# New DMA and port estimates in the planner that orders a two-layer hybrid backbone on one core

## The chip, the cores and the metric

The kernel runs on one core of a Trainium2 chip. A core has a matrix engine (TensorE, PE in the profile, with its weight loads as PEld), a vector engine (VectorE, DVE), an activation engine (ScalarE, ACT), GpSimd (POOL) and a queue processor (SyncE, SP) that issues DMA transfers here. Each takes its instructions in program order and waits on semaphores for the others. The metric is the device time of one execution in microseconds, as the median of several runs; lower is better.

## The reference, cut to what matters

Two layers work on 2048 latent tokens and 256 context tokens of width 1024. Each layer normalises its input, projects it, runs two groups of heads on the same projection (windowed softmax attention with eight heads, and a two-way mLSTM with four heads), gates both, and multiplies the joined result with one output matrix.

```python
def hybrid_layer(x, ctx, mod_x, mod_c, tables, norm_g, w_in, ..., last):
    xn = rmsnorm(x, norm_g) * (1 + scale_x) + shift_x
    cn = rmsnorm(ctx, norm_g) * (1 + scale_c) + shift_c
    aq, ak, av, az, mq, mk, mv, mo, mz, mi, mf = project(xn, w_in)
    ...
    att_x = window_ctx_attention(q, k, v, kc, vc, sink) * jax.nn.silu(az)
    cq, ck = mlstm_qk(cmq, cmk, conv_w, conv_b)
    xq, xk = mlstm_qk(mq, mk, conv_w, conv_b)
    h_ctx, ctx_state = mlstm_bidir(cq, ck, cmv, cmi + b_i, cmf + b_f, mlstm_init_state(B))
    h_lat, _ = mlstm_bidir(xq, xk, mv, mi + b_i, mf + b_f, ctx_state)
    m_x = mlstm_post(h_lat, mo, mz, head_g)
    out_x = jnp.concatenate([att_x, m_x], axis=-1) @ w_out
    x = x + gate_x * out_x
    if not last:
        ...
    return x, ctx

def reference(x, c, ctx, c_ctx, w_ada, b_ada, norm_g, w_in, ...):
    ...
    for l in range(DEPTH):
        ...
        x, ctx = hybrid_layer(...)
    return rmsnorm(x, final_g)
```

## The kernel before

Tokens are cut into 18 blocks of 128: two of context, sixteen latent. Every large product is done in three fp16 passes over high and low parts of the operands (`mm3`, line 350: 24 matmuls for one result), and the activations of a layer lie in SBUF as such pairs, transposed, in five group buffers `xt0` to `xt4`.

**The planner.** Nothing in the code is in the order in which it is issued. The class `Plan` (line 87) runs while the program is built. The work is written as generators. A *stream* yields pieces of TensorE work; a *task* carries the evacuation and the elementwise work that follow a piece. Each engine has a clock, E, V, S, G and Q for TensorE, VectorE, ScalarE, GpSimd and SP's DMA issues. `op` (line 147) estimates when an instruction starts and ends (`cost`, line 116), moves the engine's clock, notes from when on its result can be read and its buffer can be written, and then emits the real instruction (line 179; every instruction carries this line in the profile, so that one reads it by tiles). The planner's present is the clock of TensorE.

`till` (line 233) holds a stream or a task back until the estimate says that its operand is ready within 0.2 us. `get` (line 190) holds it back until the buffer it asks for is estimated free within 0.5 us, 0.2 us in PSUM. `put` (line 222) gives a buffer back with the latest time noted for it; for a buffer that a DMA reads this is the DMA's estimated landing. When all streams are held back, the clock of TensorE jumps to the earliest time that one waits for. So an estimate changes no instruction; it changes in which order the instructions of an engine come, and the engines then run in that order with real semaphores.

`run_until` (line 253) takes tasks first and then one piece of the first stream that is not held back: weight loads (priority -1), then keys and values, gates and out-projection (1), then alpha, beta and adaLN (2). Streams of one priority are sorted by the TensorE time they have used over their weight: alpha has `W_ALPHA` = 308, beta 560.

**Alpha** (line 1203) is the attention, four units of two heads in each layer. For each block of 128 queries it emits two *scores* (line 1064, one for each head), the gate projection `zproj` and, one block later, `pv` (line 1120), the product with the values; every second block also `qproj`. A score's task (line 1087) takes the row maximum on VectorE in a PSUM buffer `d` (two of them), the exponential on ScalarE, writes the high part of the probabilities to `ph` on ScalarE and the low part on VectorE, gives `d` back, and has SP transpose `ph` into `pp` by DMA. There is one buffer `ph`, for up to 1280 columns (twice five blocks of 128), and three `pp`. `ph` is free again when the transpose has landed.

**Beta** (line 1614) is the mLSTM, four heads in each layer: `mproj` (line 1210: projections, a five-tap convolution on GpSimd and VectorE, forward states) and `mmix` (line 1385: outputs in the order of the backward scan). `mmix` reads queries, gate rows and states from DRAM scratch by DMA (`p<-qD`, `mb<-mD`, `s<-cfD`).

**Joining.** The out-projection (`outproj`, line 1648) of a block needs that block's output of all heads, which goes through DRAM (`mixD`). Its weights are loaded by the stream `wo` (line 1896). It starts when beta's last `mproj` is done, when the weights of beta's last `mmix` are loaded, and when alpha's last unit has set the flag "wa soon" (line 1194), eight blocks, that is sixteen scores, before its end; it also needs the group buffers `xt4` and `xt3`, which alpha's and beta's last unit free (`clear`, line 1624). Alpha's last unit and `outproj` take the latent blocks in the same falling order. Layer 1 starts from what `outproj` of layer 0 puts into its group buffers, with DMA transposes of 2048 columns (`norm_dma`, line 675, and `prep`, line 1729).

**Lanes.** The program's DMAs take eight semaphores in turn; a DMA is issued when the one eight before it has landed.

The lines that the change touches: `__init__` (line 91), the branches of `cost` for "Q" and for VectorE (lines 124 to 145), and `op` from line 162 to line 171.

Of the kernel before, what the change touches and what calls it, by code (L numbers as in the profile page):

```python
# [7 lines left out]
F16 = mybir.dt.float16  # L8
# [5 lines left out]
P = 128  # L14
D = 1024
# [38 lines left out]
def _isap(v):  # L54
    return hasattr(v, "ap") and hasattr(v, "offset")
# [9 lines left out]
def _span(v):  # L65
    """Name and range of the bytes of one partition (or of DRAM) that v covers."""
    dims = list(v.ap)
    size = 2 if v.dtype == F16 else 4
    off = v.offset
    if v.space != bass.MemoryType.DRAM:  # L70
        step = dims[0][0]
        off = off % step if step else off
        dims = dims[1:]
    lo = hi = off
    for st, n in dims:
        if st < 0:
            lo += st * (n - 1)
        else:
            hi += st * (n - 1)
    return v.name, lo * size, (hi + 1) * size  # L80


W_ALPHA = 308.0
LAT, WAR = 0.12, 0.12


class Plan:
    """The order of emission.  Streams and tasks are generators: they yield True after a piece of work,
    a time to wait for, or None while a flag or a buffer is missing.  The engines' times are estimated."""

    def __init__(self):
        self.clk = dict(E=0.0, V=0.0, S=0.0, G=0.0, Q=0.0)
        self.dma = 0.0
        self.wr, self.rd, self.bank_of = {}, {}, {}
        self.done, self.tasks, self.streams = set(), [], []
        self.spec, self.cnt, self.rel, self.tag_of = {}, {}, {}, {}
# [4 lines left out]

# [1 line left out]
    def _times(self, table, v):  # L103
# [12 lines left out]
    def cost(self, e, name, a, kw):  # L116
# [7 lines left out]
        if e == "Q":  # L124
            b = n * a[0].shape[0] * (2 if a[0].dtype == F16 else 4)
            if name == "dma_start_transpose":
                return 0.8, 2.2 + b / 300e3
            return 0.46, 2.0 + b / 300e3
        if name == "tensor_reduce":
# [11 lines left out]
        if name == "reciprocal":  # L141
            n *= 8
        if name == "tensor_copy" and a[0].dtype == F16:
            n /= 2
        return 0.065 * (1 + min(cols, 2)) + n / 960.0, LAT

    def op(self, e, name, fn, a, kw):
# [13 lines left out]
        for v in ins + outs:  # L161
            for f, x in self.bank_of.get(v.name, {}).items():
                if f != e:
                    t = max(t, x)
        end = t + cost
        self.clk[e] = end
        see = end + lat
        if e == "Q":
            b = (lat - 2.0)
            self.dma = max(self.dma, end) + b  # L170
            see = self.dma + 2.0
        for v in outs:
# [7 lines left out]

# [1 line left out]
    def buffers(self, tag, pool, shape, dtype, bufs, psum=False):  # L182
# [17 lines left out]
    def take(self, tag, n, shape=None, dtype=None):  # L200
        """n buffers at once."""
        while True:
            if self.cnt[tag] + n > self.spec[tag][3]:
                yield None
            elif sorted(self.rel[tag])[n - 1] > self.now + 0.5:
                yield sorted(self.rel[tag])[n - 1]
            else:
                return [self.new(tag, shape, dtype) for _ in range(n)]
# [22 lines left out]

# [1 line left out]
    def till(self, *aps, slack=0.2):  # L233
# [74 lines left out]
class Kern(Plan):  # L308
# [33 lines left out]

# [1 line left out]
    def mm(self, out, lhsT, rhs, start=True, stop=True):  # L344
# [5 lines left out]
    def mm3(self, out, lh, rh, step=6):  # L350
        """Three passes over pairs: lh, rh give the operand of (hi or lo, k)."""
        c = 0
        yield from self.till(lh(0, 0), lh(1, KT - 1), rh(0, 0), rh(1, KT - 1))
        for k in range(KT):
            for a, b in ((0, 0), (0, 1), (1, 0)):
                self.mm(out, lh(a, k), rh(b, k), start=(k == 0 and a + b == 0), stop=(k == KT - 1 and a == 1))
                c += 1
                if c % step == 0 and c < 3 * KT:
                    yield True

# [1 line left out]
    def open(self, es):  # L362
# [44 lines left out]

# [1 line left out]
    def consts(self):  # L409
# [29 lines left out]

# [1 line left out]
    def scale_of(self, src, n=1, s=None, inv=None):  # L441
        """s = 2^14 / 2^floor(log2 src) and 1 / s, per partition."""
        V = self.V
# [9 lines left out]
    def pmax(self, am, out):  # L453
        """out = maximum over partitions of am [P, 1], on every partition."""
        yield from self.till(am)
# [5 lines left out]

# [1 line left out]
    def load_w(self, key, pieces, tag, scale=None, gate=(), gram=False, early=False, fast=False, space=None, into=None):  # L463
        """pieces: dram aps [D, n <= 128].  u: the product's unit.  With gram: the power of two that
        brings products of the first 128 columns under 2^15 (Cauchy-Schwarz), and u over it."""
        V, S, G, Q = self.V, self.S, self.G, self.Q
# [80 lines left out]

# [1 line left out]
    def ada(self, l, parts, width, tags):  # L549
        """Rows (g (1 + scale), shift, gate) of both streams to modD; the scale of xn."""  # L550
        A, Q, V = self.A, self.Q, self.V
# [73 lines left out]

# [1 line left out]
    def rstd(self, ss, scale, eps, n=1, out=None):  # L627
        """(ss * scale + eps) ^ -1/2 with one Newton step."""
        V, G = self.V, self.G
# [13 lines left out]
    def norm_pe(self, l, b, xr, free=None):  # L643
        """xr [P, D] of block b, normed and modulated, to the pairs XT of layer l."""
        S, V = self.S, self.V
# [29 lines left out]
    def norm_dma(self, l, b, xr, grab):  # L675
        """norm_pe with the turn done by DMA."""
        g, o = self.grp(b)
# [15 lines left out]
    def split(self, pair, x, s):  # L693
        """x times the column s as the pair of fp16 parts."""
        yield from self.till(x, s)
# [93 lines left out]

# [1 line left out]
    def rope(self, u, n, tok):  # L791
        """u [P, n] of latent tokens tok .. tok + n, turned in place."""
        V, G = self.V, self.G
# [12 lines left out]

# [1 line left out]
    def kphase(self, l):  # L808
# [67 lines left out]

# [1 line left out]
    def rphase(self, l):  # L878
# [106 lines left out]

# [1 line left out]
    def attention(self, l, j):  # L987
# [220 lines left out]

# [1 line left out]
    def mproj(self, l, h):  # L1210
# [172 lines left out]

# [1 line left out]
    def mmix(self, l, h):  # L1385
# [245 lines left out]
    def move_wo(self, l):  # L1631
        """The weights of the out-projection, from the room of the next layer's XT to their own."""
        yield from self.need(("alpha", l), ("mmix", l, MH - 1), ("wo", l, 3))
# [12 lines left out]

# [1 line left out]
    def outproj(self, l):  # L1648
# [59 lines left out]
        def scaled(gt, s):  # L1708
            """The gate with the units of the weights in it."""
            for n in range(4):  # L1710
# [34 lines left out]
        def grab(i):  # L1745
            """A buffer for a pair, and what gives it back: in the room of an XT, or a slot."""
            while True:
# [110 lines left out]

# [1 line left out]
    def loaders(self):  # L1860
# [49 lines left out]

# [1 line left out]
    def run(self):  # L1912
# [73 lines left out]
```

## Time and profile before

| what | us |
|---|---|
| median of 3 runs | 2785.13 |
| fastest and slowest run | 2782.59, 2791.67 |
| span of the profiled execution, first to last instruction | 2804.1 |

The profiled execution is one more execution of the same program, with the profiler on; its span is the only time that the profile gives for it. From first to last instruction it is 19.0 us (0.7%) longer than the median run. TensorE was granted 0.966 of its full clock on average over the span.

The page gives busy time by engine, the chain of work that ended last, and groups of instructions; a group is named by the tile that is written, "<-", and the tiles that are read. Other views show the instructions in order of time, the waits by who waited for whom, and the busy time in chosen stretches. A row of waits gives the total, how often, and the longest one. In the timeline, "[0.95 <-DMA pp<-ph]" says that the engine stood idle for 0.95 us and that the landing of the DMA from `ph` to `pp` ended it.

### The profile page before, as it was taken

What the parts mean: (1) busy time and instruction counts of PE and PEld (TensorE: products, weight loads), DVE (VectorE), ACT (ScalarE), POOL (GpSimd) and SP (SyncE); (2) the same over time, 40 slices, a digit from 0 to 9 for tenths busy, and PEclk for the clock granted to TensorE, in tenths of its full rate; (3) what the DMA queues carried; (4) which work ended last, traced back from release to release, by engine and by line L of the source; (5) the groups of instructions that cost most, each with busy time, mean ns of one, the idle gap of its engine ahead of it and who ended that gap; (6) DMA issues with size and microseconds to landing.
All of it is one profiled execution on the core that took longest, in us unless ns stands there. A gap on an engine that the chain in (4) does not pass through costs nothing. (4 is left out here: it accounts for less than half of the span.)

```text
span 2804.1 us, 64646 instructions
## 1 busy us (share of the span) xinstructions
PE 2470.3 (88%) x23650; PEld 1890.5 (67%) x23650; DVE 1850.9 (66%) x4817; ACT 1488.1 (53%) x3788; POOL 1515.6 (54%) x2832
## 2 busy tenths in 40 slices
PE   6789899988999899888799888998898899988898
PEld 2766786678668776775355558867785787677443
DVE  4878566756575656567677676657666665757775
ACT  1546565556566655565222356655674566556421
POOL 1846476637654765275322563775577367637321
PEclk8899999999999999999899999999999999999999
DMA  8344663577446634578888636633663675267775
GB/s 265 116 130 107 139 137 84 102 147 142 111 93 146 134 58 120 116 140 198 220 209 199 153 79 123 134 84 88 144 114 96 110 137 102 62 123 164 186 190 163
DMA packets 822448, 376.16 MB, mean 134 GB/s; under 512 B 492537, under 2 KB 800241, under 8 KB 821105
## 3 DMA queue, kind: packets, MB, share of 16 engines
q1 hardware_dynamic: 822128, 372.02, 59.2%
q8 instruction: 186, 3.05, 0.5%
q14 instruction: 134, 1.09, 0.1%
HBM read 198.99 MB, written 57.56 MB: 91 GB/s over the span
## 5 line engine op out<-in xcount | busy, mean ns | idle before, releaser
L179 PEld LDWEIGHTS <-xt 128*128 128x128 f16 x12048 | 901.8, 99 | 246.2 <-issue 51.0
L179 PE MATMUL b<-woz,xt 128*128 128x256 f16 (+2 forms) x3840 | 490.8, 277 | 24.8 <-DVE p L179 13.4
L179 PE MATMUL b<-xt,wqk 128*128 128x512 f16 (+1 forms) x1824 | 390.8, 367 | 1.4 <-DVE held L179 1.4
L179 DVE SCALAR_TENSOR_TENSOR ph<-d,ph 128x640 f16<-128x640 f32 (+2 forms) x272 | 212.3, 781 | 133.3 <-ACT ph L179 131.8
L179 ACT ACTIVATE d<-d,smx,un 128x640 f32<-128x640 f32 (+2 forms) x272 | 223.4, 821 | 126.4 <-DVE smx L179 113.4
L179 PEld LDWEIGHTS <-wqk 128*128 128x128 f16 x1824 | 176.9, 99 | 167.0 <-issue 11.2
L179 PE MATMUL d<-ks,toz 128*128 128x256 f16 (+1 forms) x1568 | 190.8, 258 | 92.8 <-DVE ph L179 62.8
L179 POOL TENSOR_TENSOR p<-p 128x128 f32<-128x128 f32 x272 | 128.6, 475 | 254.2 <-ACT p L179 240.5
L179 PE MATMUL b<-wa,xt 128*128 128x128 f16 (+1 forms) x3336 | 250.1, 226 | 4.0 <-ACT toz L179 3.1
L179 POOL TENSOR_TENSOR held<-held,mhalf 128x1 f32<-128x1 f32 x200 | 115.9, 580 | 240.5 <-DVE held L179 234.7
L179 PEld LDWEIGHTS <-toz 128*128 128x128 f16 x1568 | 148.1, 100 | 139.8 <-issue 54.8
L179 PE MATMUL b<-wv,xt 128*128 128x128 f16 x3456 | 228.9, 220 | 11.3 <-DVE p L179 5.3
L179 ACT ACTIVATE ph<-d 128x640 f16<-128x640 f32 (+2 forms) x272 | 182.0, 669 | 93.3 <-DMA pp<-ph 91.7
L179 DVE CUSTOM_DVE_ANT_0 d<-d,mask 128x640 f32<-128x640 f32 (+1 forms) x240 | 196.0, 817 | 36.4 <-PE d L179 35.8
L179 POOL TENSOR_TENSOR g<-g,mb 128x512 f32<-128x512 f32 (+1 forms) x152 | 189.0, 1243 | 39.4 <-ACT g L179 28.0
L179 PE MATMUL b<-xt,wa 128*128 128x256 f16 x1632 | 198.2, 275 | 4.1 <-DVE toz L179 1.9
L179 POOL TENSOR_TENSOR mb<-mb,mask 128x256 f32<-128x256 f32 x136 | 100.9, 742 | 177.0 <-DMA mb<-mD 143.5
L179 POOL TENSOR_TENSOR toz<-toz,cs 128x256 f32<-128x256 f32 x160 | 125.3, 803 | 105.3 <-DMA cs<-in_rope 83.1
L179 PEld LDWEIGHTS <-wa 128*128 128x128 f16 x1696 | 163.7, 99 | 27.2 <-issue 5.5
L179 DVE TENSOR_REDUCE held<-g 128x1 f32<-128x1024 f32 x110 | 133.1, 1212 | 62.8 <-DMA g<-mixD 34.4
L179 PE MATMUL b<-xt,xt 128*128 128x512 f16 x768 | 169.9, 382 | 5.3 <-DMA xt<-xt 3.2
L179 DVE SCALAR_TENSOR_TENSOR g<-g,cw 128x512 f32<-128x512 f32 (+1 forms) x152 | 152.4, 1002 | 31.4 <-POOL g L179 28.5
(243 smaller groups left out, 5200.1 us busy)
## 6 DMA issues: line engine op xcount, KB each, us to landing
mb<-mD SPq DMA_DIRECT2D x136, 256.0 KB
g<-in_w_in SPq DMA_DIRECT2D x60, 512.0 KB
cs<-in_rope SPq DMA_DIRECT2D x80, 256.0 KB
mixD<-p SPq DMA_DIRECT2D x272, 64.0 KB
g<-mixD SPq DMA_DIRECT2D x34, 512.0 KB
g<-in_w_ada SPq DMA_DIRECT2D x32, 512.0 KB
g<-in_x SPq DMA_DIRECT2D x24, 512.0 KB
cfD<-s SPq DMA_DIRECT2D x136, 64.5 KB
```

The source lines that it names most:

```text
L179: fn(*a, **kw)
```

## The change

It replaces estimates. No instruction, buffer, weight or priority is edited; docstrings and comments go, too.

- A plain DMA was estimated at 0.46 us of SP's time, and at 2.0 us plus its bytes over 300 GB/s from the end of the issue to the landing, transfers one behind another. It becomes 0.49 us of SP's time; the transfer may begin 0.3 us after the start of the issue and takes a time by the number and size of its contiguous runs; then 1.5 us pass to the landing where it writes DRAM, 1.9 us where it reads a kernel input, 3.6 us where it reads DRAM scratch or SBUF into SBUF.
- A DMA transpose was 0.8 us of SP's time, then 0.2 us and its bytes over 300 GB/s as a transfer, then 2.0 us. It becomes 1.2 us and 0.45 ns for each column over 512 as SP's time, a transfer of 25 ns for each column over sixteen engines, begun at the end of the issue, and 1.9 us.
- Eight DMAs are under way at most: a DMA starts no earlier than the landing of the one eight before it.
- A VectorE instruction with two operands of more than one column in SBUF, and every GpSimd instruction, exclude each other in time: the planner remembers the last six such stretches of each, and moves the start behind them.
- `tensor_tensor_reduce` (the row maximum in a score) costs 0.25 us plus a column per 960 MHz cycle, where it had 0.065 us for itself and for each column operand.

```diff
+def _run(v):
+
+    size = 2 if v.dtype == F16 else 4
+    r = size
+    for st, n in reversed(list(v.ap)):
+        if n == 1:
+            continue
+        if st * size != r:
+            break
+        r *= n
+    return r
+
+
+def _move(out, in_):
+
+    b = 2 if out.dtype == F16 else 4
+    for d in out.shape:
+        b *= d
+    r = max(min(_run(out), _run(in_), 4096), 4)
+    return b / r * (10 + 0.0447 * r) / 16e3
+
+
+def _base(out, in_):
+
+    if out.space == bass.MemoryType.DRAM:
+        return 1.5
+    return 1.9 if in_.name.startswith("in_") else 3.6
+
+
+def _two(a, kw):
+
+    n = 0
+    for v in list(a[1:]) + [v for k, v in kw.items() if k != "accum_out"]:
+        n += _isap(v) and _free(v) > 1 and v.space != bass.MemoryType.PSUM
+    return n > 1
...
         self.dma = 0.0
+        self.lanes, self.port = [0.0] * 8, dict(V=[], G=[])
...
         if e == "Q":
-            b = n * a[0].shape[0] * (2 if a[0].dtype == F16 else 4)
             if name == "dma_start_transpose":
-                return 0.8, 2.2 + b / 300e3
-            return 0.46, 2.0 + b / 300e3
+                return 1.2 + max(n - 512, 0) * 0.00045, 1.9 + n / 128 * 128 * 25e-3 / 16
+            return 0.49, _base(a[0], a[1]) + _move(a[0], a[1])
...
+        if name == "tensor_tensor_reduce":
+            return 0.25 + n / 960.0, LAT
...
+        if e == "Q":
+            t = max(t, self.lanes.pop(0))
+        elif e == "G" or (e == "V" and _two(a, kw)):
+            other = self.port["V" if e == "G" else "G"]
+            for p, q in other:
+                if p <= t < q:
+                    t = q
+            self.port[e] = self.port[e][-5:] + [(t, t + cost)]
         end = t + cost
         self.clk[e] = end
         see = end + lat
         if e == "Q":
-            b = (lat - 2.0)
-            self.dma = max(self.dma, end) + b
-            see = self.dma + 2.0
+            turn = name == "dma_start_transpose"
+            base = 1.9 if turn else _base(a[0], a[1])
+            self.dma = max(self.dma, end if turn else t + 0.3) + lat - base
+            see = max(self.dma + base, end)
+            self.lanes.append(see)
```

## The prediction, made before the changed kernel was timed

> **What bounds the kernel now.** I read the page first (span, engines, chain), then TensorE's waits, then the time of one score in the timeline, then what the last out-projection starts on.
>
> ```profile
> span 2804.1 us, 64646 instructions
> PE 2470.3 (88%) x23650; PEld 1890.5 (67%) x23650; DVE 1850.9 (66%) x4817; ACT 1488.1 (53%) x3788; POOL 1515.6 (54%) x2832
> PE b L179 6%; DMA pp<-ph 3%; DMA mb<-mD 2%; DMA g<-mixD 2%; DVE g L179 1%; DVE held L179 1%; POOL mb L179 1%; DMA g<-in_w_in 1%; PE d L179 1%; SPq L179 1%; POOL g L179 1%; DVE ph L179 1%; DVE xt L179 1%; POOL p L179 1%; ACT d L179 1%
> ```
>
> TensorE is the busiest engine, and 2804 - 2470 = 334 us of its span are idle. No estimate can save more than these. Of all transfers the attention's transpose (`pp<-ph`) has the largest part of the chain. The waits of TensorE say what the idle time is:
>
> ```profile
> PE d L179 <- DVE ph L179: 62.8, 67, 4.5
> PE b L179 <- DMA pp<-ph: 29.5, 28, 2.3
> PE d L179 <- DVE toz L179: 26.9, 12, 4.5
> PE b L179 <- DMA p<-qD: 19.0, 8, 4.7
> ```
>
> The planner holds a piece back until it believes the operand ready, so each such wait is an estimate that was too early. The first two, 62.8 + 29.5 = 92 us, belong to a score's tail: a buffer `d` is given back by the instruction that writes the low half of `ph`, and `pv` needs `pp`. Behind both stands the single buffer `ph`:
>
> ```profile
> ACT ph L179 <- DMA pp<-ph: 91.7, 83, 3.3
> ```
>
> ```profile
> L179 SPq DMA_TRANSPOSE pp<-ph x272: 1189/1342/6842, 205.0 to 2737.4; - x136
> ```
>
> In 83 of 272 scores ScalarE came to write `ph` before the transpose of the score before had landed. The timeline shows one such cycle:
>
> ```profile
> 1963.23 0.70 ACT L179 ACTIVATE ph<-d 128x640 f16<-128x640 f32 x1 [0.95 <-DMA pp<-ph]
> 1963.96 0.82 DVE L179 SCALAR_TENSOR_TENSOR ph<-d,ph 128x640 f16<-128x640 f32 x1 [1.30 <-ACT ph L179]
> 1964.85 1.32 SPq L179 DMA_TRANSPOSE pp<-ph  x1
> 1967.90 0.70 ACT L179 ACTIVATE ph<-d 128x640 f16<-128x640 f32 x1 [0.97 <-DMA pp<-ph]
> ```
>
> From one write to the next 4.67 us pass, and from the issue to the landing 1967.90 - 1964.85 = 3.05 us.
>
> How fast do scores come on average, and who waits for them? Stages of both layers, counted by the instructions on `ph` (start and end, length, VectorE's and ScalarE's time and count; 144 scores in layer 0, so 128 in layer 1); then what ends beta and starts the output weights and the out-projection (`b<-xt,g` and `b<-xt,xt` with 512 columns), one view after the other:
>
> ```profile
> 201.00:1219.00 1018.00, 101.55 (x134) 87.19 (x134) 0.98 0.56 116
> 201.00:1325.00 1124.00, 109.44 (x144) 94.01 (x144) 0.98 0.58 121
> 1645.00:2533.00 888.00, 90.88 (x113) 78.13 (x114) 0.97 0.54 109
> 1645.00:2598.00 953.00, 96.60 (x120) 82.64 (x120) 0.97 0.55 113
> ```
>
> ```profile
> 1218.73 1.67 SPq L179 DMA_DIRECT2D g<-in_w_out  x2
> ...
> 2532.62 1.21 SPq L179 DMA_DIRECT2D g<-in_w_out  x2
> ```
>
> ```profile
> 1305.18 0.39 PE L179 MATMUL b<-s,mb 128*128 128x129 f32 x2
> 1309.78 10.53 PE L179 MATMUL b<-xt,g 128*128 128x512 f16 x48 [1.98 <-DMA g<-g]
> ...
> 2598.14 0.39 PE L179 MATMUL b<-s,mb 128*128 128x129 f32 x2
> ...
> 2611.59 2.71 PE L179 MATMUL b<-xt,xt 128*128 128x512 f16 x6
> ```
>
> A score takes 888 / 113 = 7.86 us in layer 1. There the first output weights are fetched after 113 of 128 scores: the flag "wa soon" comes sixteen scores before the end, so in layer 1 alpha releases them. The chain just before that is made of transposes:
>
> ```profile
> 2489.82 8.45 DMA pp<-ph
> ...
> 2508.26 5.53 DMA pp<-ph
> ...
> 2521.61 6.30 DMA pp<-ph
> ...
> 2533.26 6.73 DMA g<-in_w_out
> ```
>
> In layer 0 the weights come after 134 of 144 scores, some 5 after the flag (128, and one that is planned ahead), so alpha has 5 x 1018 / 134 = 38 us to spare there.
>
> **The change, part by part.** Every instruction stays, so the direct cost is nothing; all of it is order.
>
> *Transposes.* For 1280 columns the old estimate from issue to landing is 0.8 + 0.2 + 1.09 + 2.0 = 4.09 us; the new one is 1.55 + 2.0 + 1.9 = 5.45 us. The undisturbed landing above took 3.05 us, a delayed one 5.53 to 8.45. So the new number moves away from the undisturbed case by 1.36 us, toward the crowded one. The two parts of it are added where the trace overlaps them: the issue takes 1.32 us and all is landed 1.7 us after it. The planner gives `ph` back at the estimated landing, so the shortest cycle between two scores that it allows becomes 1.36 us longer (ScalarE's and VectorE's part is planned at 0.43 + 0.12 + 0.73 + 0.12 = 1.40, so 5.5 before and 6.85 now, where the chip did 4.67). Transposes of 2048 columns go from 4.75 to 6.99 us; those are pipelined over several blocks in the out-projection, whose stage has little idle TensorE time, and I cost them at nothing; if that cover fails, each layer's join gains one 2.2 us.
>
> *Scratch reads and stores.* `mb<-mD` lies on the chain with these times from issue to release:
>
> ```profile
> 2014.77 5.04 DMA mb<-mD
> 2038.50 4.93 DMA mb<-mD
> ```
>
> The old estimate is 0.46 + 0.87 + 2.0 = 3.33 us, the new one 0.3 + 1.05 + 3.6 = 4.95: here the change is right, and the 19.0 us that TensorE waits for `p<-qD` can go as well.
>
> *Gain.* A later `ph`, `pp` and `p<-qD` in the plan let TensorE do another piece first, and 92 + 19 = 111 us are what that can return. Much remains, since the landing of a transpose varies from 3.05 to 8.45 us around any one number. I take a little over half, 60 us, 30 for each layer; the bounds are 0 and 111. [...]
>
> *Loss.* Where alpha is behind its share it is taken first whenever it isn't held back, and then the cycle of `ph` is its pace. How much of the 1.36 us enters the mean of 7.86? The upper end is 1.36 less the real wait that goes, 91.7 / 272 = 0.34, so +1.0; the lower end is 0, where something else than `ph` sets the pace. Since 4.67 of 7.86 us are the buffer's own cycle and 83 of 272 scores, about a third, met it, I take a third: +0.35, a pace of 8.2 us.
>
> What is late next? Alpha falls behind beta, and the end of a layer has scores left with nothing beside them. A score costs TensorE, by these rows,
>
> ```profile
> 2600.08 1.01 PE L179 MATMUL b<-vp,pp 128*128 128x128 f16 x20
> 2601.93 2.78 PE L179 MATMUL b<-xt,wa 128*128 128x256 f16 x24 [0.83 <-DVE p L179]
> 2604.54 0.71 PE L179 MATMUL d<-ks,toz 128*128 128x256 f16 x6
> 2605.09 1.50 PE L179 MATMUL b<-wa,xt 128*128 128x128 f16 x24
> ```
>
> 0.71 + (1.01 + 1.50) / 2 + 2.78 / 4 = 2.66 us. In layer 1 beta now ends 953 us after alpha's start with 120 scores done. With 30 us of waits gone, at pace p, beta ends at T = 953 - 30 - 2.66 (120 - T / p): for p = 8.2, T = 894 with 109 scores done. The 4 to the flag then run alone at 4.67 each: 913 us, against 888 now, 25 us later. From the first fetch to the first product it is 2611.59 - 2532.62 = 79 us, of which I estimate 10 saved with beta's transfers out of the way. So layer 1 starts its out-projection 15 us later. In layer 0, with beta's end at 1305 - 201 = 1104 and about 141 scores done by then (144 by 1325), T = 1035 with 126 done; 3 more to the flag (at 129) give 1048 us against 1018, 30 later, less 10, and less some 10 of a stretch that is idle anyway:
>
> ```profile
> 1320.00:1360.00 40.00, 22.65 (x103) 9.69 (x101) 26.58 (x48) 9.72 (x14) 15.60 (x19) 0.82 1.03 287
> ```
>
> (40 us of span, 22.65 of TensorE; the DMA share there is 1.03.) Sum: 15 + 10 = **+25 us**.
>
> *Eight under way.* Ten transfers are issued between these two, both counted:
>
> ```profile
> 2524.54 0.50 SPq L179 DMA_DIRECT2D s<-cfD  x1
> ...
> 2535.93 0.50 SPq L179 DMA_DIRECT2D s<-cfD  x1
> ```
>
> So nine steps take 11.4 us and eight 10.1, more than the longest landing above, 8.45. I cost the limit at nothing; the start, where loads come faster, has 201 us and no alpha or beta.
>
> *VectorE beside GpSimd.* The planner now puts an instruction with two SBUF operands behind a whole run of GpSimd instructions, up to six. The trace has a tiny one (minimum, median and maximum in ns):
>
> ```profile
> L179 DVE TENSOR_TENSOR col<-smx x136: 116/161/2104, 217.4 to 2749.9; 128x2 f32<-128x2 f32 x136
> ```
>
> Its median is 45 ns over its minimum, its longest 2.0 us over. So the planned wait is mostly too long, for alpha and beta alike. The wait that hangs most on such instructions is TensorE's for `toz` (rotary positions, then the split of the queries), 26.9 us: gone or doubled, the bounds are -27 and +27. By the median I take 0.
>
> **Rivals.**
> *The waits go and the tails stay covered: faster.* If the pace stays at 7.86 because beta's share sets it, T in layer 1 is 913 us with 116 scores done, and the flag comes before beta's end. Layer 1 gains 10 us by the shorter fetch, layer 0 its 30: -40 us, and about -70 with every wait gone. It speaks for it that layer 0 has 38 us to spare; against it, that layer 1 has none. It decides below a pace of about 8.0 us.
> *The full lengthening: clearly slower.* At 8.86 us, T = 863 with 97 scores; 16 alone give 936, 48 later and 38 after the shorter fetch; layer 0 has T = 999, 113 scores, 16 alone, 1075, 57 later, 37 after both reductions: +75 us.
> *The order hardly changes.* Gain and tail cancel within 0.3% (8 us, about what a measurement of this kernel can tell from no change).
>
> **How the numbers follow.** Forecast, a modest lag of alpha (+9 to +50 us): 0.38. Full lag (+50 to +90): 0.12. Faster rival (-9 to -70): 0.36. Cancelled: 0.14. The +25 us refer to the profiled span, 2804 to 2829; on the median run of 2785.13, 19 us lower, that is 2810 us. Range: 8 in 10 cases lie between -55 and +80 us, 2730 to 2865; the likeliest case alone is 2794 to 2835. Faster 0.36, same 0.14, slower 0.50.
>
> **What would show it.** Right: ScalarE's wait on `pp<-ph` falls well under 91.7 us and TensorE's on `ph` and `pp` under 40; scores per stage in 1645 to 2533 us fall below 113; beta's last product comes earlier, the first `w_out` fetch of layer 1 later than 2533, with idle TensorE between the two. Wrong: the fetch comes earlier with the waits gone (the faster rival), or the waits stay as they are, which would mean that the landing's spread and not its mean makes them.

## The result, and the profile after

| kernel | median, us | profiled span, us | ratio to before (95% interval) |
|---|---|---|---|
| before | 2784.71 (2782.59 to 2791.67, 4 runs) | 2804.1 | 1 |
| after | 2958.14 (2954.09 to 2964.16, 4 runs) | 2954.9 | 1.0616 [1.0595, 1.0636] |

The change costs 173 us by the medians and 151 us between the two profiled executions. That is the forecast direction, but outside the range. The differences between stages below are those of the profiled executions; where the other 22 us lie is not shown. Times below are medians, ratios are against the kernel before on the same chip. Of `e2_turn_only` below, one of two executions was in a slower state, so it has a time but no interval.

The page after (span, TensorE's busy time, its granted clock in 40 slices, the chain by line; the planner's lines have moved, so every row now says L228):

```profile
span 2954.9 us, 64915 instructions
...
PE 2519.8 (85%) x23650; PEld 1932.4 (65%) x23650; DVE 1884.0 (64%) x4817; ACT 1497.8 (51%) x3788; POOL 1498.6 (51%) x2832
...
PEclk8899999999999999667999899999999999766999
...
PE b L228 20%; DMA pp<-ph 3%; DVE g L228 2%; PE d L228 2%; POOL g L228 1%; DMA xt<-xt 1%; DVE held L228 1%; DVE ph L228 1%; POOL mb L228 1%; POOL held L228 1%; ACT d L228 1%; POOL p L228 1%; ACT ph L228 1%; DVE toz L228 1%; ACT g L228 1%
```

The same 23650 matmuls take 2519.8 us where they took 2470.3, and TensorE's idle time is 2954.9 - 2519.8 = 435 us where it was 334. So 49 of the 151 us are slower matmuls and 101 are more idle time. The clock row shows where: two dips, in the 17th to 19th and the 35th to 37th slice, one at the end of each layer's alpha.

The waits after (us, times, longest):

```profile
PE d L228 <- DVE ph L228: 106.7, 63, 4.7
...
ACT ph L228 <- DMA pp<-ph: 73.3, 56, 5.2
...
PE b L228 <- DMA pp<-ph: 49.0, 29, 7.7
```

ScalarE's wait fell a little (91.7 to 73.3), and both waits of TensorE that the change was expected to shorten rose, from 62.8 and 29.5. The table of stages says why. Layer 0 from alpha's first write to `ph` on VectorE to beta's last product, then from there to the out-projection, and the same for layer 1 (start and end, length, busy time and count of PE, PEld, DVE, ACT, POOL, granted clock, DMA share, GB/s):

```profile
208.00:1174.00 966.00, 907.36 (x9573) 757.77 (x9571) 622.58 (x1756) 587.05 (x1623) 643.34 (x1232) 0.98 0.55 118
1174.00:1336.00 162.00, 88.05 (x817) 73.20 (x816) 95.40 (x247) 71.18 (x162) 24.42 (x42) 0.66 0.49 108
1728.00:2524.00 796.00, 742.04 (x7920) 626.41 (x7920) 511.82 (x1459) 503.66 (x1383) 531.95 (x1045) 0.98 0.54 112
2524.00:2724.00 200.00, 110.39 (x961) 90.56 (x961) 108.67 (x286) 82.36 (x191) 29.70 (x54) 0.66 0.39 90
```

The same cuts before; the stretches behind beta are 5 and 14 us there:

```profile
205.00:1305.00 1100.00, 988.37 (x10499) 818.88 (x10499) 701.88 (x2014) 660.13 (x1800) 647.44 (x1257) 0.98 0.58 120
1305.00:1310.00 5.00, 1.81 (x27) 1.40 (x26) 4.86 (x15) 3.46 (x10) 3.49 (x5) 1.00 0.97 201
...
1656.00:2598.00 942.00, 835.66 (x9045) 704.60 (x9044) 616.56 (x1728) 581.23 (x1570) 572.03 (x1087) 0.97 0.56 115
2598.00:2612.00 14.00, 7.29 (x88) 6.24 (x87) 13.59 (x39) 9.79 (x25) 11.21 (x25) 0.99 0.54 122
```

Beta's stage is shorter by 134 and 146 us, and TensorE idles in it for 58.6 and 54.0 us instead of 111.6 and 106.3: the waits did go. Behind beta a tail of 162 and 200 us has appeared, in which TensorE works 54 and 55% of the time at a clock of 0.66. How many scores lie there (VectorE's and ScalarE's instructions on `ph` in the same stretches):

```profile
208.00:1174.00 966.00, 85.15 (x114) 72.58 (x113) 0.98 0.55 118
1174.00:1336.00 162.00, 18.95 (x23) 16.05 (x23) 0.66 0.49 108
1728.00:2524.00 796.00, 76.61 (x95) 64.67 (x94) 0.98 0.54 112
2524.00:2724.00 200.00, 21.84 (x27) 18.52 (x27) 0.66 0.39 90
```

Beside beta 114 and 95 scores are done, one in 966 / 114 = 8.47 and 796 / 95 = 8.38 us. In the tails 23 and 27 follow, one in 7.0 and 7.4 us. A last 7 and 6 run beside the out-projection. Before, 141 (and one more right at the cut) and 120 were done by the same mark, one in 7.75 and 7.85 us:

```profile
205.00:1305.00 1100.00, 107.66 (x141) 92.44 (x141) 0.98 0.58 120
1656.00:2598.00 942.00, 96.57 (x120) 82.05 (x119) 0.97 0.56 115
```

TensorE's waits in beta's stage of layer 1, before and after:

```profile
PE d L179 <- DVE ph L179: 30.9, 39, 2.5
PE b L179 <- DMA pp<-ph: 20.8, 17, 2.3
...
PE b L179 <- DMA p<-qD: 4.5, 2, 2.5
```

```profile
PE d L228 <- DVE ph L228: 14.2, 18, 2.3
...
PE b L228 <- DMA pp<-ph: 5.0, 5, 3.0
PE b L228 <- DMA p<-qD: 3.2, 2, 2.3
```

and from 2524 to 2780 us, the tail and the last scores:

```profile
PE d L228 <- DVE ph L228: 39.7, 14, 4.7
...
PE b L228 <- DMA pp<-ph: 16.1, 9, 3.5
```

What such a tail looks like (timeline of layer 1; other instructions left out):

```profile
2645.28 0.83 DVE L228 SCALAR_TENSOR_TENSOR ph<-d,ph 128x640 f16<-128x640 f32 x1 [1.17 <-ACT ph L228]
...
2646.25 1.05 PE L228 MATMUL d<-ks,toz 128*128 128x256 f16 x6 [2.87 <-DVE ph L228]
...
2647.34 0.83 DVE L228 CUSTOM_DVE_ANT_0 d<-d,mask 128x640 f32<-128x640 f32 x1 [1.24 <-PE d L228]
...
2648.64 0.86 ACT L228 ACTIVATE d<-d,smx,un 128x640 f32<-128x640 f32 x1 [3.39 <-DVE smx L228]
...
2649.51 0.69 ACT L228 ACTIVATE ph<-d 128x640 f16<-128x640 f32 x1
...
2649.95 4.42 PE L228 MATMUL b<-xt,wa 128*128 128x256 f16 x24
2650.24 0.82 DVE L228 SCALAR_TENSOR_TENSOR ph<-d,ph 128x640 f16<-128x640 f32 x1 [1.70 <-ACT ph L228]
...
2654.03 1.21 SPq L228 DMA_DIRECT2D g<-in_w_out  x2
...
2658.16 0.82 DVE L228 SCALAR_TENSOR_TENSOR ph<-d,ph 128x640 f16<-128x640 f32 x1 [1.17 <-ACT ph L228]
...
2659.04 0.72 PE L228 MATMUL d<-ks,toz 128*128 128x256 f16 x6 [2.78 <-DVE ph L228]
```

Each engine waits for the one before it: the low half of `ph` frees `d`, the score fills it, VectorE takes the maximum, ScalarE the exponential, and only then comes the write to `ph`. On ScalarE the exponential of the next score stands ahead of the write to `ph` of this one in 222 of 270 pairs of the trace, against 164 before, and in 54 of 61 in the tails and the last scores behind them. A projection of 24 matmuls (4.42 us here at a granted clock of 0.62, 2.78 at 1.00 in the row of the prediction) stands in that chain on TensorE. The first output weights of layer 1 are fetched at 2654.03 us, 926 us after alpha's start (the same mark as above), where it was 877.

All of the profiled difference, by the stretches between the same marks: the start +3; layer 0 from alpha to the out-projection 1105 to 1128, +23; from there to alpha of layer 1, 346 to 392, +46; layer 1 from alpha to the out-projection 956 to 997, +41; the last out-projection 193 to 230, +37. Sum +150. With alpha's start of layer 1 taken at its first matmul of a score instead (1651.3 and 1716.7 us), the +46 and +41 become +39 and +48.

The last out-projection, where no alpha is left, shows its own change of order. VectorE before and after (other rows left out):

```profile
2694.86 1.22 DVE L179 TENSOR_REDUCE held<-g 128x1 f32<-128x1024 f32 x1 [0.98 <-DMA g<-mixD]
...
2700.05 1.28 DVE L179 SCALAR_TENSOR_TENSOR g<-g,held,xt 128x1024 f32<-128x1024 f32 x1 [0.23 <-POOL held L179]
...
2706.19 1.22 DVE L179 TENSOR_REDUCE held<-g 128x1 f32<-128x1024 f32 x1 [1.80 <-DMA g<-mixD]
```

```profile
2843.92 1.28 DVE L228 SCALAR_TENSOR_TENSOR g<-g,held,xt 128x1024 f32<-128x1024 f32 x1 [1.75 <-POOL held L228]
2845.12 1.21 DVE L228 TENSOR_REDUCE held<-g 128x1 f32<-128x1024 f32 x1
...
2855.75 1.28 DVE L228 SCALAR_TENSOR_TENSOR g<-g,held,xt 128x1024 f32<-128x1024 f32 x1 [1.75 <-POOL held L228]
2856.95 1.21 DVE L228 TENSOR_REDUCE held<-g 128x1 f32<-128x1024 f32 x1
```

Before, the row maximum of a later block (`held<-g`) comes first, as soon as its load has landed, and the final norm of an earlier block (`g<-g,held,xt`) after it. Now the maximum stands behind that norm, which waits for GpSimd. Averaged over the last ten blocks, one takes 13.3 us, against 11.4 before.

### The profile page after: what moved, and what is told of

Read it like the earlier page. It is cut to its first block, busy times and chain, and to the rows that moved or that the text cites. A ratio compares the mean times of both kernels' runs of the same rounds, so it can differ in the third digit from the quotient of the medians.

```text
span 2954.9 us, 64915 instructions
## 1 busy us (share of the span) xinstructions
PE 2519.8 (85%) x23650; PEld 1932.4 (65%) x23650; DVE 1884.0 (64%) x4817; ACT 1497.8 (51%) x3788; POOL 1498.6 (51%) x2832
## 3 DMA queue, kind: packets, MB, share of 16 engines
q8 instruction: 186, 3.05, 0.4%
## 5 line engine op out<-in xcount | busy, mean ns | idle before, releaser
L228 PEld LDWEIGHTS <-xt 128*128 128x128 f16 x12000 | 907.8, 101 | 251.8 <-issue 53.8
L228 PE MATMUL b<-woz,xt 128*128 128x256 f16 (+2 forms) x3824 | 468.7, 276 | 15.2 <-DMA xt<-xt 11.4
L228 PE MATMUL b<-xt,wqk 128*128 128x512 f16 (+1 forms) x1824 | 381.7, 363 | 2.7 <-DVE wqk L228 2.7
L228 POOL TENSOR_TENSOR p<-p 128x128 f32<-128x128 f32 x272 | 128.7, 475 | 475.0 <-ACT p L228 434.7
L228 PE MATMUL d<-ks,toz 128*128 128x256 f16 (+1 forms) x1568 | 200.8, 267 | 147.0 <-DVE ph L228 106.7
L228 DVE SCALAR_TENSOR_TENSOR ph<-d,ph 128x640 f16<-128x640 f32 (+2 forms) x272 | 212.7, 782 | 142.7 <-ACT ph L228 141.5
L228 ACT ACTIVATE d<-d,smx,un 128x640 f32<-128x640 f32 (+2 forms) x272 | 223.5, 822 | 144.4 <-DVE smx L228 128.3
L228 PEld LDWEIGHTS <-wqk 128*128 128x128 f16 x1824 | 175.1, 98 | 167.9 <-issue 3.7
L228 POOL TENSOR_TENSOR held<-held,mhalf 128x1 f32<-128x1 f32 x200 | 119.6, 599 | 321.8 <-DVE held L228 301.3
L228 PEld LDWEIGHTS <-toz 128*128 128x128 f16 x1568 | 151.2, 102 | 194.8 <-DVE ph L228 65.5
L228 PE MATMUL b<-wa,xt 128*128 128x128 f16 (+1 forms) x3328 | 247.7, 232 | 1.1 <-DVE s L228 1.1
L228 DVE CUSTOM_DVE_ANT_0 d<-d,mask 128x640 f32<-128x640 f32 (+1 forms) x240 | 196.5, 819 | 78.0 <-PE d L228 77.1
L228 PE MATMUL b<-wv,xt 128*128 128x128 f16 x3456 | 223.6, 220 | 9.5 <-ACT V L228 4.8
L228 ACT ACTIVATE ph<-d 128x640 f16<-128x640 f32 (+2 forms) x272 | 181.5, 667 | 74.4 <-DMA pp<-ph 73.3
L228 PE MATMUL b<-xt,wa 128*128 128x256 f16 x1632 | 214.9, 295 | 2.0 <-DVE s L228 1.9
L228 POOL TENSOR_TENSOR toz<-toz,cs 128x256 f32<-128x256 f32 x160 | 120.3, 773 | 179.3 <-DMA cs<-in_rope 111.0
L228 POOL TENSOR_TENSOR g<-g,mb 128x512 f32<-128x512 f32 (+1 forms) x152 | 192.4, 1266 | 33.1 <-ACT g L228 19.3
L228 PE MATMUL b<-xt,xt 128*128 128x512 f16 x768 | 181.3, 399 | 29.6 <-ACT d L228 17.6
L228 PEld LDWEIGHTS <-wa 128*128 128x128 f16 x1696 | 175.1, 106 | 34.3 <-issue 2.5
L228 PE MATMUL b<-vp,pp 128*128 128x128 f16 (+1 forms) x2560 | 155.4, 219 | 49.3 <-DMA pp<-ph 49.0
L228 PEld LDWEIGHTS <-pp 128*128 128x128 f16 x2560 | 140.5, 106 | 64.1 <-DMA pp<-ph 55.0
L228 DVE SCALAR_TENSOR_TENSOR g<-g,cw 128x512 f32<-128x512 f32 (+1 forms) x152 | 153.6, 1011 | 39.1 <-POOL g L228 36.2
```

The source lines that it names most:

```text
L228: fn(*a, **kw)
```

## The experiments

All edits are to the planner, against the kernel after, unless said otherwise; every kernel computes all of the reference. The "left" scores are those after beta's last product, in layer 0 and layer 1; "block" is the mean of the last ten blocks of the last out-projection. In some kernels beta's last product comes after the out-projection's first (by 29 us in layer 0 of `e1_turn_old`, by 118 us in layer 1 of `g2_two_ph_mix_old_turn`); their stage of beta then holds out-projection work, too.

### Which estimate costs the time

`e1_turn_old` sets the transposes' estimate back and keeps the rest:

```diff
             if name == "dma_start_transpose":
-                return 1.2 + max(n - 512, 0) * 0.00045, 1.9 + n / 128 * 128 * 25e-3 / 16
+                return 0.8, 2.2 + n * a[0].shape[0] * (2 if a[0].dtype == F16 else 4) / 300e3
...
-            base = 1.9 if turn else _base(a[0], a[1])
+            base = 2.0 if turn else _base(a[0], a[1])
```

The other three start from the kernel before and take one part of the change each: `e2_turn_only` the transposes' estimate, `e3_plain_only` that of the other DMAs (`_base` and `_move`), `e4_port_only` VectorE beside GpSimd with the row maximum's cost. Eight under way was not tried by itself.

> The changed kernel with the DMA transpose alone estimated as before (0.8 us of SP's time, 4.09 us in all for 1280 columns); plain DMAs, the eight lanes and the port stay as changed. Theory A (the transpose's estimate holds `ph` in the plan, alpha lags, the tails run alone: about 76 of the 150 us, and more with the slower clock there): beta and alpha end together again in both layers, within 20 us; about 2840 us, what is left being the slower out-projection. Theory B (plain scratch reads planned later do it, alpha's and the out-projection's): stays above 2900 us with the tails as they are. Theory C (VectorE's planned waits behind runs of GpSimd make alpha late): also above 2900 us, tails as they are.

> The kernel before with only the DMA transpose estimated as in the change. Theory A: most of the loss is here, 2860 to 2920 us, beta's last product in layer 1 at least 60 us before alpha's last score. Theory B and theory C: within 20 us of before, 2785.

> The kernel before with only the plain DMAs estimated as in the change (issue 0.49, begin 0.3, runs, 1.5, 1.9 or 3.6 us). Theory A: alpha and beta end together as before; the out-projection of layer 1 takes 13.5 us for a block where it took 11.4, since the row maximum of the next block is planned 1.2 us later and comes behind the final norm on VectorE: +35 to +50 us, 2820 to 2835. Theory B: both, 2880 or more, with tails. Theory C: no change, 2785, the blocks at 11.4 us.

> The kernel before with only the exclusion of VectorE and GpSimd and the new cost of the row maximum. Theory A and theory B: within 20 us of before, 2785, either way. Theory C: alpha late by it, 2850 us or more, with beta ending 60 us or more before alpha in a layer.

| kernel | median, us | ratio | left | TensorE idle in beta's stages, us | block, us |
|---|---|---|---|---|---|
| before, beside the four below | 2787.06 | 1 | 2, 8 | 112, 106 | 11.4 |
| after | 2958.14 | 1.0616 [1.0595, 1.0636] | 30, 33 | 59, 54 | 13.3 |
| e1_turn_old | 2789.54 | 1.0001 [0.9984, 1.0017] | 2, 13 | 78, 76 | 13.7 |
| e2_turn_only | 2915.79 | | 23, 32 | 82, 74 | 11.2 |
| e3_plain_only | 2839.01 | 1.0176 [1.0135, 1.0217] | 2, 10 | 98, 101 | 13.7 |
| e4_port_only | 2803.34 | 1.0065 [1.0031, 1.0098] | 6, 13 | 98, 93 | 11.3 |

With the old number for the transposes the whole loss is gone, and with the new one alone most of it is there (2916 against 2787, +129 us). The tails follow that one estimate: 2 scores are left in layer 0 and 13 in layer 1 in `e1_turn_old`, 23 and 32 in `e2_turn_only`. `e1_turn_old` came 50 us below what was expected of it: its out-projection is as slow as expected (223 us from its first product to the end, 193 before), but TensorE idles 34 and 30 us less than before in beta's stages, so the other estimates gain there what they lose in the out-projection. The other parts cost 52 and 16 us when they come alone, so the parts don't add up: 129 + 52 + 16 = 197, against 173. In `e1_turn_old` the tail of layer 1 (scores on `ph`, stage and tail):

```profile
1628.00:2510.00 882.00, 92.48 (x115) 78.49 (x114) 0.98 0.55 114
2510.00:2564.00 54.00, 5.73 (x7) 4.88 (x7) 0.65 0.60 138
```

Seven scores in 54 us are 7.7 us each, at a granted clock of 0.65. So the price of a score alone is no work of the new estimate; the estimate only sets how many are left.

### Through the single buffer, or through alpha's share

The theory: the planner holds `ph` back for longer than the chip does. Rival: alpha simply gets too small a share beside beta. `f1_two_ph` gives `ph` two buffers, and makes room for it with one `toz` and three `p` fewer; `f2_weight` raises alpha's weight.

```diff
-        B("toz", m, [P, 2, P], F32, 8)
-        B("p", m, [P, P], F32, 15)
+        B("toz", m, [P, 2, P], F32, 7)
+        B("p", m, [P, P], F32, 12)
...
-        B("ph", at, [P, 1280], F16, 1)
+        B("ph", at, [P, 1280], F16, 2)
```

```diff
-W_ALPHA = 308.0
+W_ALPHA = 500.0
```

> The changed kernel with two buffers `ph` in place of one; for their room `toz` has 7 buffers instead of 8 and `p` 12 instead of 15. Estimates as changed. Theory A: the cycle of `ph` no longer binds in the plan, alpha keeps up, fewer than 12 scores are left when beta ends, and most of the 150 us are back: 2780 to 2850 us, the out-projection of layer 1 still at 13.5 us for a block. Rival (the late landing hurts through `pp` and `pv`, not through `ph`): no gain, 2930 us or more.

> The changed kernel with alpha's weight 500 in place of 308. Theory A (alpha is held back by the estimate of `ph`, not by its share): nothing to gain, 2935 to 2975 us, some 26 to 34 scores left in each layer when beta ends. Rival (the new estimates only unbalance the shares, and the weight was fitted to the old ones): the tails go, 2860 us or less.

| kernel | median, us | ratio | left |
|---|---|---|---|
| f1_two_ph | 2776.88 | 0.9949 [0.9929, 0.997] | 0, 0 |
| f2_weight | 2953.59 | 1.0593 [1.0553, 1.0633] | 30, 33 |

The weight does nothing: the scores left are the same to the number, so alpha's share is not what holds it back. The second buffer takes back everything, with the same estimates. The scores of layer 1 in `f1_two_ph`, all inside beta's stage:

```profile
1652.00:2548.00 896.00, 102.65 (x128) 87.06 (x126) 0.98 0.57 122
```

896 / 128 = 7.0 us, faster than the 7.85 of before, so the estimate acted through the one buffer. (The fewer `toz` and `p` were not tried by themselves; alpha's own pace rose, which fewer buffers don't explain.) The second one alone is not what gains: with the estimates of before it is slower than before (`g3_old_two_ph` below).

### Is the undisturbed landing the right number

`f4_meas_mix` plans a transpose as the undisturbed one of the prediction ran, with the landing counted from the issue's start (1280 columns: 0.3 + 2.0 + 0.75 = 3.05 us), and `g<-mixD` with a base of 2.4 instead of 3.6 us. `g4_mix` is its control, with the new transposes and the same base for `g<-mixD` (the second edit below).

```diff
-                return 1.2 + max(n - 512, 0) * 0.00045, 1.9 + n / 128 * 128 * 25e-3 / 16
+                return 0.33 + n * 0.00078, 0.75 + n * 25e-3 / 16
...
-            base = 1.9 if turn else _base(a[0], a[1])
-            self.dma = max(self.dma, end if turn else t + 0.3) + lat - base
+            base = 0.75 if turn else _base(a[0], a[1])
+            self.dma = max(self.dma, t + 0.3 if turn else t + 0.3) + lat - base
```

```diff
 def _base(out, in_):
...
+    if "mixD" in in_.name:
+        return 2.4
```

> The changed kernel with the transpose estimated as the trace has it when nothing disturbs it (1.33 us of SP's time and 3.05 us to the landing for 1280 columns, 1.93 and 4.25 for 2048: transfer begun 0.3 us after the issue, 0.75 us behind it), and `mixD` loads as in f3_old_turn_mix. Theory A: no tail in either layer, since the planned cycle of `ph` is 4.5 us; about as f3_old_turn_mix or better, 2740 to 2770. Rival (a late estimate is what removes TensorE's waits in the middle): more waits on `ph` and `pp` than before, 2780 to 2810.

> The changed kernel with `mixD` loads alone planned as in f3_old_turn_mix. The out-projection's part by itself: layer 1 from 13.3 to 11.4 us a block, 25 to 35 us less, 2920 to 2935; the tails as they are, 26 or more scores in each layer. If the blocks stay at 13 us, 2950 or more.

`f4_meas_mix` takes 2829.51 us (1.0149 [1.0121, 1.0176]), `g4_mix` 2955.18 (1.0573 [1.0539, 1.0607]), and the same with the old transposes, `f3_old_turn_mix` of the next part, 2765.18. So `f4_meas_mix` is slower than both of the times expected of it. With 3.05 us no score is left at beta's end, but the other fault returns: TensorE idles 115 and 122 us in beta's stages, and ScalarE, which now comes too early, waits for

```profile
ACT ph L230 <- DMA pp<-ph: 296.9, 176, 6.6
```

where `f3_old_turn_mix` (4.09 us) has

```profile
ACT ph L230 <- DMA pp<-ph: 145.5, 114, 3.7
```

and `g4_mix` (5.45 us) 64.8. Of these three numbers the middle one is best. It is neither the undisturbed landing nor a crowded one, but the one nearest to the middle of the landings that the trace shows: before, 156 transposes can be told because some engine waited for them, and from issue to landing they took 2.3 to 9.3 us (some have fewer than 1280 columns), half of them under 4.4.

### The out-projection

`f3_old_turn_mix` is `e1_turn_old` with the smaller base for `g<-mixD` of the part above; `h1_plain_old` is the kernel after with the old estimate for all DMAs that are no transposes; `h2_no_port` is the kernel after without VectorE beside GpSimd and the row maximum's cost. The edits of the last two:

```diff
-            return 0.49, _base(a[0], a[1]) + _move(a[0], a[1])
+            return 0.46, 2.0 + n * a[0].shape[0] * (2 if a[0].dtype == F16 else 4) / 300e3
...
-            base = 1.9 if turn else _base(a[0], a[1])
-            self.dma = max(self.dma, end if turn else t + 0.3) + lat - base
+            base = 1.9 if turn else 2.0
+            self.dma = max(self.dma, end if turn else end) + lat - base
```

```diff
-        if name == "tensor_tensor_reduce":
-            return 0.25 + n / 960.0, LAT
...
-        elif e == "G" or (e == "V" and _two(a, kw)):
+        elif False:
```

> As e1_turn_old (all of the change but the transpose's estimate), and loads from `mixD` planned with 2.4 us after the transfer instead of 3.6, about their old estimate. Theory A, with the out-projection's loss in the later planned load: layer 1's blocks come back from 13.7 to 11.4 us, 30 us less than e1_turn_old: 2750 to 2765 us, faster than before. Rival (the blocks are slow by the other estimates there, residual loads and stores): no change, 2790.

> The changed kernel with all plain DMAs estimated as before (transpose, lanes and port as changed). If the plain estimates as a whole make the out-projection's blocks slow, and not the one for `mixD` alone, layer 1 goes back to 11.4 us a block; the tails stay (25 or more scores), so 2900 to 2930 us. If the blocks stay above 13 us, something else in the change does it too, and it is 2940 or more.

> The changed kernel without the exclusion of VectorE and GpSimd and with the old cost of the row maximum (transpose, plain DMAs and lanes as changed). If the exclusion keeps the next block's row maximum behind the final norm on VectorE, 11.4 us a block and 2920 us or less; if it is the plain estimates, 13.3 us or more as changed and 2935 to 2975, tails as they are.

| kernel | median, us | ratio | left | block, us |
|---|---|---|---|---|
| f3_old_turn_mix | 2765.18 | 0.9916 [0.9886, 0.9945] | 2, 13 | 11.4 |
| g4_mix | 2955.18 | 1.0573 [1.0539, 1.0607] | 30, 33 | 13.4 |
| h1_plain_old | 2923.5 | 1.0459 [1.0417, 1.05] | 28, 32 | 11.3 |
| h2_no_port | 2957.48 | 1.058 [1.0539, 1.0621] | 26, 32 | 13.3 |

The block is 11.2 to 11.5 us wherever the plain DMAs keep their old estimate, also beside new transposes (`h1_plain_old`, `e2_turn_only`), and 13.3 to 13.7 with the new one in after, `e1_turn_old`, `e3_plain_only` and `h2_no_port`. VectorE in `h1_plain_old` shows the order of before again:

```profile
2801.77 1.22 DVE L228 TENSOR_REDUCE held<-g 128x1 f32<-128x1024 f32 x1 [0.57 <-DMA g<-mixD]
...
2803.66 1.26 DVE L228 SCALAR_TENSOR_TENSOR g<-g,held,xt 128x1024 f32<-128x1024 f32 x1
...
2813.38 1.21 DVE L228 TENSOR_REDUCE held<-g 128x1 f32<-128x1024 f32 x1
```

The maximum comes first and waits for its load. Of this one load the new estimate is 0.3 + 1.55 + 3.6 = 5.45 us, the old one 0.46 + 1.75 + 2.0 = 4.21, and the chain of before shows 5.01; a base of 2.4, 4.25 in all, brings the old pace back in `f3_old_turn_mix`. It doesn't beside the new transposes (`g4_mix`, 13.4 us against 11.4, and the transposes' estimate is the only difference), nor beside the shorter ones of `f4_meas_mix` (13.1). So with the new plain DMAs the transposes' estimate counts as well. By which order on the engines it does so stays open.

### A version that beats both

Two buffers for `ph` as in `f1_two_ph`, with the smaller base for `g<-mixD` (`g1_two_ph_mix`), with that and the old transposes (`g2_two_ph_mix_old_turn`), and with all estimates of before (`g3_old_two_ph`).

> The changed kernel with two buffers `ph` (as f1_two_ph) and `mixD` loads planned as in f3_old_turn_mix; the transpose as changed. If tail and out-projection are two separate losses, both go: f1_two_ph less some 30 us, 2740 to 2755 us. If the out-projection's blocks depend on more than that load's estimate, as in f4_meas_mix (13.1 us a block with it), 2765 to 2785.

> As g1_two_ph_mix, with the transpose estimated as before. With two buffers its estimate should matter little: within 15 us of g1_two_ph_mix. If the late estimate still costs or saves through `pp`, more than that.

> The kernel before, all estimates as before, with two buffers `ph` (`toz` 7, `p` 12). If the single buffer costs the kernel before too (ScalarE's 91.7 us on it), 2740 to 2775 us; if the estimate of 4.09 us already hides it, 2780 to 2795.

| kernel | median, us | ratio | left | TensorE idle in beta's stages, us | block, us |
|---|---|---|---|---|---|
| g1_two_ph_mix | 2775.23 | 0.993 [0.9907, 0.9953] | 0, 0 | 87, 78 | 13.6 |
| g2_two_ph_mix_old_turn | 2733.08 | 0.98 [0.9758, 0.9842] | 0, 0 | 84, 101 | 11.5 |
| g3_old_two_ph | 2819.4 | 1.0087 [1.0055, 1.012] | 0, 0 | 115, 113 | 11.5 |

`g2_two_ph_mix_old_turn` is the fastest kernel of the study, 2.0% under before. Against `g3_old_two_ph` it has the new plain DMAs (but for the one load), eight under way and VectorE beside GpSimd: these are worth 86 us once neither the buffer nor the out-projection gives them back; which of the three brings it was not tried. Against `g1_two_ph_mix` it differs in the transposes' estimate alone, and that still costs 42 us with two buffers, more than the 15 expected: the last out-projection takes 224 us in `g1_two_ph_mix` and 195 in `g2_two_ph_mix_old_turn`. The trace before has the transposes of 2048 columns (`xt<-xt`) landing 4.3 us after the start of their issue (the middle one of the 23 that can be told); the new estimate for them is 6.99 us, the old one 4.75.

## Why the prediction was wrong in size and right in sign

- **Mechanism: right.** The transposes' estimate lengthens the planned cycle of the single `ph`, alpha falls behind beta, and scores are left to run alone. `e1_turn_old` and `f1_two_ph` each cut the chain at one link (the second with fewer `toz` and `p` besides) and the loss is gone. The signs named ahead are there: fewer scores beside beta, an earlier end of beta, a later fetch of the weights with idle TensorE behind. One sign failed: TensorE's waits on `ph` and `pp` were to fall under 40 us. They did within beta's stages (12.9 + 2.7 us in layer 0, 14.2 + 5.0 in layer 1), but the tails have waits of their own, and the sums rose.
- **Gain: right for the waits that it counts, too small for the idle time.** 60 us were taken, 30 for each layer. In beta's stages the waits on `ph`, `pp` and `p<-qD` fell together from 49.4 to 28.3 us in layer 0 and from 56.2 to 22.4 in layer 1, so by 55 us. All of TensorE's idle time there fell by 112 - 59 = 53 and 106 - 54 = 52 us: other waits shrank as well (that of `b` for VectorE's `p` from 41 to 4 us in both layers), and the stages are shorter.
- **Pace: mis-sized.** A third of 1.36 us was taken, 8.2 us. It was 8.47 and 8.38, against 7.75 and 7.85 before: 0.72 and 0.53, about half. The bounds, 0 and 1.0, held.
- **TensorE's price of a score: mis-sized, too small.** 2.66 us, put together from four groups of matmuls. By the stages' busy times it is (988.4 - 907.4) / 28 = 2.9 in layer 0 (28 scores fewer) and (835.7 - 742.0) / 25 = 3.7 in layer 1; the second holds 15 us of matmuls with `wv`, which are beta's and which the kernel after does ahead of the mark. By the tiles that are alpha's alone (`ks`, `pp`, `wa`) it is 83.0 / 28 = 3.0 and 82.6 / 25 = 3.3. The four rows miss no matmul: they hold 34 for a score, and in layer 0 these tiles have 32 for each score fewer. The projections (`wa`) take longer there, 1.75 us for a score against 1.45 by the rows. With gain and pace as measured, the prediction's own formula, T = 942 - 52 - price (120 - T / 8.38), gives 836 us in layer 1 at 2.66 and 815 at 3.3; beta ended after 796, with the `wv` matmuls on the other side of the mark. 95 scores were done by then, not 109.
- **"Run alone at 4.67 each": the step that failed within the layers.** 4.67 us was a cycle of `ph` with other work around it. Alone a score takes 7.0 and 7.4 us, 7.7 in `e1_turn_old`, since its chain passes through PE, DVE and ACT one by one and includes a projection at a lower clock (4.42 us at 0.62 in the timeline, against 2.78 at 1.00). With 95 scores done after 796 us, the 18 up to the fetch of the output weights took 926 - 796 = 130 us; at 4.67 each they would have taken 84, and the fetch would have come 3 us later than before instead of 49. That the order on ScalarE makes a score alone that long is read from the timeline and was not tried by itself. From the first fetch to the first product it took 2724.5 - 2654.0 = 70 us, and 69 were forecast.
- Together: layer 1 from alpha to its out-projection +41 us instead of +15, layer 0 +23 instead of +10. The earlier end of beta paid for most of the long tails.
- **What stood at nothing in the sum: the step that failed outside, and the larger part.** The prediction costs the transposes of 2048 columns at nothing, calls the plain DMAs' new estimate right and gives it no loss, and has no term for the out-projections. The 46 us from the first out-projection to alpha of layer 1 and the 37 of the last out-projection were both 0 in the sum; with the 3 us of the start they are 86 of the 126 us missed. For the last one the cause is shown: the plain DMAs' estimate, which I took as right because it is near the measured landing, moves the row maximum behind another block's norm, as the rows of before, after and `h1_plain_old` show (`h1_plain_old`: 197 us from its first product to the end, `e2_turn_only` 200, before 193, after 230). For the 46 us it is not: with `e1_turn_old` 27 remain, with `e2_turn_only` 22, with `e3_plain_only` 7, with `f1_two_ph`, without any late score, 37.
- **Scratch reads: half right.** TensorE's wait on `p<-qD` fell from 19.0 to 15.9 us after, but to 2.2 in `e1_turn_old`. A better number there did not buy time as long as the transposes' number stood.
- **VectorE beside GpSimd at 0: within its bounds.** +16 us alone, nothing that can be told within the whole change (1.058 [1.0539, 1.0621] without it, 1.0616 [1.0595, 1.0636] with it).
- The rival of the full lengthening had nearly the right number of scores left (31 in each layer, where 30 and 33 came), but the same 4.67 us for a score alone and nothing for the out-projection, so its +75 us fell short as well.

## What to carry to other kernels

A planner's estimate of a transfer that holds the only buffer of its kind is also a rate limit: check what the planned cycle becomes against the cycle that the trace shows, and try a second buffer before the number is tuned. A number nearer to a measured landing is not by itself better (the load of `mixD` takes 5.01 us on the chain, and 5.45 planned gives a slower kernel than 4.25), since what counts is which instruction it puts ahead of which on an engine (with the row maximum behind the norm a block of the last out-projection took 13.3 us, ahead of it 11.4); change one estimate at a time. When a forecast leaves work to "run alone", price it from a stretch where it does run alone, and don't put a stage at zero because the change is not aimed at it.

## What the runs showed of the hardware

In the kernel after, the granted clock was 0.98 in beta's stages, where TensorE was busy 93 to 94% of the time, and 0.66 in both tails, where it was busy 54 and 55%; 24 matmuls of 256 columns took 4.42 us in the second tail, at 0.62, where they took 2.78 us before, at 1.00. So a tail pays twice, in idle time and in slower matmuls (TensorE's busy time is 49 us higher in all). TensorE's longest idle gap was 3.5 and 3.0 us in beta's two stages, and 5.5 and 10.8 us in the tails; the trace has the clock at half 6 and 7 times in the stages, 34 us in all in each, and 8 and 12 times in the tails, 109 us of 162 and 136 of 200. No run here varied the idle gaps or the busy share alone, so what brings the clock down was not shown.

The issue of a transpose on SyncE's queue took no longer after the change (minimum, median and maximum in ns; before 1189/1342/6842):

```profile
L228 SPq DMA_TRANSPOSE pp<-ph x272: 1190/1337/4081, 208.4 to 2772.5; - x136
```

The landing is another matter: of the 156 transposes before that can be told, the issue took under 1.36 us in half of the cases and at most 6.8, and from its end to the landing it was 1.1 to 5.9 us. So both vary, and any one number for the sum is often wrong by more than a microsecond (the middle one, 4.35 us, by that much in 82 of the 156).
